# The feed-forward products of a hybrid block by Strassen's scheme: seven block products in place of eight

## The chip, the cores and the metric

The kernel runs on one core of a Trainium2 chip. The metric is the device time of one execution in microseconds, as the median of three runs. A core has a tensor engine (PE), a vector engine (DVE), a scalar engine (ACT) and a general engine (POOL), each with an instruction queue of its own that is worked off in order, and a queue for transfers (SP). All four engines work on the on-chip memory SBUF. PE writes its products to PSUM, from where DVE and ACT read them.

## The reference

A stack of two layers works on 512 tokens of 1024 features. Each layer has a feed-forward part (FFN), a mixer and a second FFN:

```python
def rms_norm(x, w):
    xf = x.astype(jnp.float32)
    y = xf * lax.rsqrt(jnp.mean(xf * xf, axis=-1, keepdims=True) + NORM_EPS)
    return (y * w.astype(jnp.float32)).astype(x.dtype)

def swiglu_ffn(x, w_gate, w_up, w_down):
    return (jax.nn.silu(x @ w_gate) * (x @ w_up)) @ w_down

for l in range(DEPTH):
    x = x + 0.5 * swiglu_ffn(rms_norm(x, ffn1_norm_w[l]), ffn1_w_gate[l], ffn1_w_up[l], ffn1_w_down[l])
    x = x + hybrid_mixer(rms_norm(x, mix_norm_w[l]), ...)
    x = x + 0.5 * swiglu_ffn(rms_norm(x, ffn2_norm_w[l]), ffn2_w_gate[l], ffn2_w_up[l], ffn2_w_down[l])
```

The hidden width of an FFN is 2816. The mixer joins an mLSTM, a state-space model and a differential attention. Everything is float32.

## The kernel before, in words

The residual stream x lies feature-major: eight tiles x[d] of 128 features by 512 tokens. A float32 product is made of three products of a faster kind (float32r). Each operand is split into a high part, which is its cast, and a low part, which is the rest; `mm3` (lines 125 to 128) adds high x high, high x low and low x high into one PSUM bank. `prep` splits x (lines 133 and 134: xh, xl) and multiplies the norm's gain in; the root mean square is divided out behind the product. Weights come by `load` (1 MiB each, two buffers `raw`) and are split by `split` in pieces of 1024 columns: ACT casts to `whi` (line 120), DVE subtracts to `wlo` (line 121).

`ffn` runs over 22 tiles f of the hidden width. For each it makes gate and up (8 steps of k each, so 24 products of 128x128 by 128x512 each), then DVE and ACT form silu(gate) * up and split it into gh and gl (lines 203 to 214). Then it runs over the eight output tiles d, with 22 steps of k each, and adds to x[d] (line 227). POOL has nothing to do in an FFN. In the first FFN `build_bias` makes a table for the attention, which one transfer from POOL's queue writes to the chip's main memory (line 252).

A scheduler sets the order in each queue when the program is built; blocks under `tc.high_priority()` (loads and splits) go ahead where they can. A tile waits for its slot, which the pool's number of buffers (`bufs`) and its `tag` decide.

## Time and profile before

| what | value |
|---|---|
| median of 3 runs | 2030.84 us (2029.91 to 2032.18) |
| span of the profiled execution | 2028.7 us |
| busy PE | 1990.6 us, 98% |
| busy DVE, ACT, POOL | 50%, 35%, 5% |
| mean granted clock of PE | 0.992 |

The span runs from the first to the last instruction of the profiled execution; its time in the runs is 2.1 us more in the median. Busy time of PE is the union of its products, which overlap: one lasts longer than the distance to the next start. The start-to-start distance tells what one costs in a row of them. In the rows below, "L121" is line 121 of the kernel, "wlo<-raw,whi" are output and inputs, and a bracket behind a row is the idle time of the engine ahead of it and what ended it. The duration of a DVE or POOL instruction is from its start to its end in the record, with any time that it stood inside.

### The profile page before, as it was taken

How to read it: one execution, taken by the hardware profiler on the slowest of the kernel's cores; microseconds unless marked ns; L12 is line 12 of the kernel's file. 1: busy time of each engine (PE TensorE's matmuls, PEld its weight loads, DVE VectorE, ACT ScalarE, POOL GpSimd, SP SyncE). 2: the span in 40 equal slices, each digit the busy share in tenths (PEclk: the TensorE clock that was granted, in tenths of full speed). 3: DMA queues.
4: the chain of work that ended last, by engine and by line, in shares of the span. 5: the costliest groups of instructions: out<-in, count | busy, mean ns of one | idle time of the engine just before them, and what ended most of it. 6: DMA issues, size and time to landing. Idle time of an engine off the chain costs nothing.

```text
span 2028.7 us, 23646 instructions
## 1 busy us (share of the span) xinstructions
PE 1990.6 (98%) x9654; PEld 1662.2 (82%) x9654; DVE 1014.5 (50%) x1659; ACT 700.9 (35%) x1144; POOL 110.1 (5%) x133
## 2 busy tenths in 40 slices
PE   8999999999899999999999999999998999999999
PEld 6878888978788888888888888889787888888887
DVE  6444433478766444443344444333876754444321
ACT  5223222345554333222232332223464533332211
POOL 0000000132210000000000000001222100000000
PEclk9999999999999999999999999999998999999999
DMA  5332222344212222222222222223532022222321
GB/s 177 95 118 83 104 103 85 118 144 127 83 52 81 86 104 85 103 104 83 104 84 103 104 84 104 103 75 122 159 110 88 32 99 89 104 85 103 109 99 62
DMA packets 35064, 200.73 MB, mean 99 GB/s; under 512 B 5179, under 2 KB 5467, under 8 KB 14092
## 3 DMA queue, kind: packets, MB, share of 16 engines
q1 hardware_dynamic: 29756, 185.28, 26.2%
q0 software_dynamic: 5200, 13.95, 2.8%
q8 instruction: 75, 1.23, 0.2%
q14 instruction: 33, 0.27, 0.0%
HBM read 191.56 MB, written 7.65 MB: 98 GB/s over the span
## 4 chain that ended last, share of the span: by engine, by line
PE 92%; DVE 4%; DMA 3%; ACT 1%; issue 1%; SPq 0%; POOL 0%; ACTq 0%; DVEq 0%; POOLq 0%
PE acc L126 16%; PE acc L128 16%; PE acc L127 16%; PE aux L126 12%; PE aux L128 12%; PE aux L127 12%; DMA raw<-wgu 3%; PE aux L764 1%; PE aux L643 1%; PE po L555 1%; PE po L755 0%; PE aux L544 0%; PE aux L523 0%; PE side L755 0%; ACT whi L120 0%
## 5 line engine op out<-in xcount | busy, mean ns | idle before, releaser
L120 ACT CAST whi<-raw 128x1024 fp32r<-128x1024 f32 (+2 forms) x344 | 350.8, 1022 | 994.2 <-PE acc L127 407.3
L121 DVE TENSOR_TENSOR wlo<-raw,whi 128x1024 fp32r<-128x1024 f32 (+1 forms) x326 | 386.2, 1187 | 346.1 <-ACT whi L120 345.6
L126 PE MATMUL acc<-xh,whi 128*128 128x512 f32 x896 | 353.1, 394 | 12.8 <-ACT xh L133 8.2
L127 PE MATMUL acc<-xl,whi 128*128 128x512 f32 x896 | 352.5, 393 | 0.0
L128 PE MATMUL acc<-xh,wlo 128*128 128x512 f32 x896 | 352.3, 393 | 0.1
L126 PE MATMUL aux<-xh,whi 128*128 128x512 f32 x704 | 274.2, 389 | 0.0
L128 PE MATMUL aux<-xh,wlo 128*128 128x512 f32 x704 | 274.1, 389 | 0.0
L127 PE MATMUL aux<-xl,whi 128*128 128x512 f32 x704 | 274.1, 389 | 0.0
L126 PEld LDWEIGHTS acc<-xh,whi 128*128 128x128 f32 x896 | 169.4, 189 | 47.3 <-ACT xh L133 8.2
L128 PEld LDWEIGHTS acc<-xh,wlo 128*128 128x128 f32 x896 | 169.1, 189 | 34.7 <-DVE wlo L121 1.1
L127 PEld LDWEIGHTS acc<-xl,whi 128*128 128x128 f32 x896 | 169.4, 189 | 34.0 <-DVE xl L134 0.4
L207 DVE TENSOR_TENSOR us<-aux,rsb 128x512 f32<-128x512 f32 x88 | 60.8, 691 | 265.7 <-PE aux L128 265.7
L127 PEld LDWEIGHTS aux<-xl,whi 128*128 128x128 f32 x704 | 132.3, 188 | 27.6
L128 PEld LDWEIGHTS aux<-xh,wlo 128*128 128x128 f32 x704 | 132.3, 188 | 27.5
L126 PEld LDWEIGHTS aux<-xh,whi 128*128 128x128 f32 x704 | 132.3, 188 | 27.4
L204 DVE TENSOR_TENSOR gs<-acc,rsb 128x512 f32<-128x512 f32 x88 | 60.8, 691 | 176.4 <-PE acc L128 172.5
L126 PE MATMUL acc<-gh,whi 128*128 128x512 f32 x352 | 138.7, 394 | 0.0
L126 PE MATMUL aux<-gh,whi 128*128 128x512 f32 x352 | 138.7, 394 | 0.0
L128 PE MATMUL acc<-gh,wlo 128*128 128x512 f32 x352 | 138.0, 392 | 0.0
L128 PE MATMUL aux<-gh,wlo 128*128 128x512 f32 x352 | 138.0, 392 | 0.0
L127 PE MATMUL acc<-gl,whi 128*128 128x512 f32 x352 | 136.6, 388 | 0.0
L127 PE MATMUL aux<-gl,whi 128*128 128x512 f32 x352 | 136.6, 388 | 0.0
(265 smaller groups left out, 2668.4 us busy)
## 6 DMA issues: line engine op xcount, KB each, us to landing
raw<-wgu SPq DMA_DIRECT2D x87, 1024.0 KB, 4.8
raw<-wdn SPq DMA_DIRECT2D x44, 1024.0 KB, 4.8
raw<-win SPq DMA_DIRECT2D x12, 1024.0 KB, 4.9
raw<-winf SPq DMA_DIRECT2D x12, 1024.0 KB, 4.9
raw<-wout SPq DMA_DIRECT2D x8, 1024.0 KB, 4.8
st<-qk_dram POOLq DMA_DIRECT2D x24, 256.0 KB, 5.4
qk_dram<-hl POOLq DMA_DIRECT2D x16, 256.0 KB, 3.3
sS<-row_dram SPq DMA_DIRECT2D x8, 512.0 KB, 4.4
```

What stands on the lines that cost most here:

```text
L120: act.copy(hi[:, t], raw[:, lo:lo + n])
L121: eng.tensor_tensor(lw[:, t], raw[:, lo:lo + n], hi[:, t].bitcast(F32), ALU.subtract)
L126: pe.matmul(out, lh, rh, start=first, stop=False)
L127: pe.matmul(out, lh, rl, start=False, stop=False)
L128: pe.matmul(out, ll, rh, start=False, stop=last)
L204: dve.tensor_tensor(gs, pp[0], rsb, ALU.mult)
L207: dve.tensor_tensor(us, pp[1], rsb, ALU.mult)
L555: pe.matmul(po[:, h * 64:(h + 1) * 64], at["a", n][:, j * P:(j + 1) * P], dv[j][:, (2 * p + h) * 64:(2 * p + h + 1) * 64], start=j == 0, s ...
L643: pe.matmul(py[:, j * P + hh * 64:j * P + hh * 64 + 64], sS[:, hh * S + j * P:hh * S + (j + 1) * P], XC[:, j, h * 64:(h + 1) * 64], start= ...
L764: pe.matmul(pnv[:, n, :], D[:, off[j] + (n - j) * P:off[j] + (n - j + 1) * P], V[:, j, h, :], start=j == 0, stop=j == n)
```

## The change

Gate, up and down products are made as products of 2x2 blocks. A block is 128 features by 128 hidden features (of a weight matrix) or 128 rows by 256 tokens (of x or of the hidden values h). A product of two such 2x2 arrays takes eight block products; the scheme takes seven, with sums of blocks as operands (the form with few sums by Winograd). The seven are named in STEPS: 11, s1, s2, s4, s3, 12, 22. The weights' operands are the loaded blocks 11, 12, 22 and the sums s1 = 21 + 22, s2 = s1 - 11, s3 = 11 - 21, s4 = 12 - s2, which POOL makes (`form`), 1024 columns each, in a pool of three buffers. Each of the seven is then split as before. The moving operands are three blocks of x and four sums of blocks (xR, xT, made by `prep7`), or of h (hR, hT, made behind each pair of hidden tiles, with POOL for the sums). Each product is 256 columns wide.

`gate_up(p)` makes the pair p of hidden tiles (11 pairs), gate and up in turn in each step. PSUM results are added on: ACT copies four of the seven running sums out (sn), and DVE and POOL add them to the outputs. `down(c, j)` makes half j of the output features from the chunk c of three pairs (two in the last), and adds to x with small instructions on DVE and POOL. Chunks run between the pairs: down(0, .) behind pair 3, down(1, .) behind pair 6, down(2, 0) behind pair 9, and the rest at the end.

`load` now brings 512 KiB in four buffers, one per block; whi and wlo have four buffers in place of three. In the mixer loads are cut the same way and some tiles move to other slots. `build_bias` takes its tiles from the slots "cg" and "cu" of the FFN, where "cu" has one buffer.

```diff
     def load(src, soon=True):
         n = src.shape[1]
         with tc.high_priority() if soon else nullcontext():
-            raw = wp.tile([P, 2 * WPC], F32, name="raw", tag="raw", bufs=2)
+            raw = wp.tile([P, WPC], F32, name="raw", tag="raw", bufs=4)
             nc.sync.dma_start(out=raw[:, :n], in_=src)
         return raw
 
...
     def split(raw, lo, n, eng=dve):
-            hi = wp.tile([P, WPC], F32R, name="whi", tag="whi", bufs=3)
-            lw = wp.tile([P, WPC], F32R, name="wlo", tag="wlo", bufs=3)
+            hi = wp.tile([P, WPC], F32R, name="whi", tag="whi", bufs=4)
+            lw = wp.tile([P, WPC], F32R, name="wlo", tag="wlo", bufs=4)
+            act.copy(hi[:, :n], raw[:, lo:lo + n])
+            eng.tensor_tensor(lw[:, :n], raw[:, lo:lo + n], hi[:, :n].bitcast(F32), ALU.subtract)
...
+    def prep7(i, wcol, tmp, four):
+        if i == 0:
+            parts["xR"] = [handed(4 + n, [P, 4, 2, 256], F32R, f"xR{n}") for n in range(3)]
+            parts["xT"] = []
+        xT = handed(i, [P, 4, 2, 256], F32R, "xT")
+        parts["xT"].append(xT)
+        xw = four("xw")
+        for n in range(2):
+            w = pv[:, wcol + 2 * i + n:wcol + 2 * i + n + 1]
+            act.activation(xw[:, 2 * n:2 * n + 2].rearrange("p a b -> p (a b)"), x[2 * i + n], AF.Copy, scale=w)
+        for n, b in enumerate((0, 2, 3)):
+            r = parts["xR"][n][:, i]
+            act.copy(r[:, 0], xw[:, b])
+            dve.tensor_tensor(r[:, 1], xw[:, b], r[:, 0].bitcast(F32), ALU.subtract)
+        sums(four("xt"), xw, xT, dve)
+        for n in range(2):
+            square(2 * i + n, tmp)
+    def sums(t, b, out, eng):
+        eng.tensor_tensor(t[:, 0], b[:, 1], b[:, 0], ALU.subtract)
+        eng.tensor_tensor(t[:, 1], b[:, 3], t[:, 0], ALU.subtract)
+        eng.tensor_tensor(t[:, 2], b[:, 3], b[:, 1], ALU.subtract)
+        eng.tensor_tensor(t[:, 3], b[:, 2], t[:, 1], ALU.subtract)
+        act.copy(out[:, :, 0], t)
+        dve.tensor_tensor(out[:, :, 1], t, out[:, :, 0].bitcast(F32), ALU.subtract)
...
-    def ffn(l, which, nxt, first):
...
+    STEPS = (("11", 0, "X"), ("s1", 3, "Y"), ("s2", 4, "X"), ("s4", 2, "Y"), ("s3", 5, "X"), ("12", 1, "Z"), ("22", 6, "X"))
+    def seven(raws, n, pair_w, np_, spool, fpool, rhs, done, after=None):
+        forms = {}
+        def form(name):
+            if name in raws:
+                src = raws[name]
+            else:
+                a, b, op, eng = {
+                    "s1": (raws["21"], raws["22"], ALU.add, pool),
+                    "s2": (forms.get("s1"), raws["11"], ALU.subtract, pool),
+                    "s4": (raws["12"], forms.get("s2"), ALU.subtract, pool),
+                    "s3": (raws["11"], raws["21"], ALU.subtract, pool),
+                }[name]
+                with tc.high_priority():
+                    src = spool.tile([P, WPC], F32, name=name, tag="S", bufs=3)
+                    eng.tensor_tensor(src[:, :n], a[:, :n], b[:, :n], op)
+                forms[name] = src
+            return split(src, 0, n)
+        ps, copies = {}, {}
+        nk = pair_w // P
+        for name, f, where in STEPS:
+            hi, lw = form(name)
+            for s in range(np_):
+                new = (s, where) not in ps
+                if new:
+                    ps[s, where] = acc() if where == "X" else aux()
+                out = ps[s, where][:, 0:256]
+                for k in range(nk):
+                    c = slice(s * pair_w + k * P, s * pair_w + (k + 1) * P)
+                    r = rhs(f, k)
+                    mm3(out, hi[:, c], lw[:, c], r[:, 0], r[:, 1], new and k == 0, k == nk - 1, True)
+                if name in ("11", "s1", "s2", "s3"):
+                    t = fpool.tile([P, 256], F32, name="sn", tag="sn", bufs=8)
+                    act.copy(t, out)
+                    copies[s, name] = t
+                done(s, name, out, copies)
+            if after:
+                after(name)
+    def ffn(l, which, nxt, first, ctx3):
+        wcol = l * PV_N + (PV_N2 if which else PV_N1)
+        fp = ctx3.enter_context(tc.tile_pool(name=f"f{l}{which}", bufs=1, reuse_waits="tile"))
...
+        def gate_up(p):
+            raws = raw11 if first and p == 0 else {b: load(aps["wgu"][l, which, p, n]) for n, b in ((0, "11"), (2, "21"), (3, "22"), (1, "12"))}
+            c = [four("cg"), fp.tile([P, 4, 256], F32, name="cu", tag="cu")]
+            def done(s, name, out, copies):
+                if name == "s4":
+                    dve.tensor_tensor(c[s][:, 1], out, copies[s, "s2"], ALU.add)
+                elif name == "s3":
+                    pool.tensor_tensor(c[s][:, 3], copies[s, "s3"], copies[s, "s1"], ALU.add)
+                elif name == "12":
+                    dve.tensor_tensor(c[s][:, 0], out, copies[s, "11"], ALU.add)
+                elif name == "22":
+                    act.copy(c[s][:, 2], out)
+            def after(name):
+                if p == 0 and name == "s1":
+                    spread(rms_of_x())
+            seven(raws, 1024, 512, 2, fp, fp, x_of, done, after)
+            cg, cu = c
+            flat = [t.rearrange("p (m n) t -> p m (n t)", m=2) for t in c]
+            rb = rsb[:, None, :].broadcast_to([P, 2, S])
+            dve.tensor_tensor(flat[0], flat[0], rb, ALU.mult)
+            pool.tensor_tensor(flat[1], flat[1], rb, ALU.mult)
+            act.activation(cg, cg, AF.Silu)
+            dve.scalar_tensor_tensor(cu, cg, 0.5, cu, ALU.mult, ALU.mult)
+            hR = fp.tile([P, 3, 2, 256], F32R, name="hR", tag="hR", bufs=4)
+            hT = fp.tile([P, 4, 2, 256], F32R, name="hT", tag="hT", bufs=4)
+            act.copy(hR[:, 0, 0], cu[:, 0])
+            act.copy(hR[:, 1:3, 0], cu[:, 2:4])
+            dve.tensor_tensor(hR[:, 0, 1], cu[:, 0], hR[:, 0, 0].bitcast(F32), ALU.subtract)
+            dve.tensor_tensor(hR[:, 1:3, 1], cu[:, 2:4], hR[:, 1:3, 0].bitcast(F32), ALU.subtract)
+            sums(four("ht"), cu, hT, pool)
+            hF[p] = hR, hT
+        def down(c, j):
+            ps = range(3 * c, min(3 * c + 3, 11))
+            n = len(ps) * P
+            src = aps["wd3"][l, which, c, j] if c < 3 else aps["wd2"][l, which, j]
+            raws = {b: load(src[m]) for m, b in ((0, "11"), (2, "21"), (3, "22"), (1, "12"))}
+            def h_of(f, k):
+                hR, hT = hF[ps[k]]
+                return hR[:, f] if f < 3 else hT[:, f - 3]
+            L, R = slice(0, 256), slice(256, 512)
+            def done(s, name, out, copies):
+                xa, xb = x[2 * (2 * j + s)], x[2 * (2 * j + s) + 1]
+                if name == "11":
+                    pool.tensor_tensor(xa[:, L], xa[:, L], copies[s, "11"], ALU.add)
+                elif name == "s1":
+                    pool.tensor_tensor(xb[:, R], xb[:, R], copies[s, "s1"], ALU.add)
+                elif name == "s2":
+                    pool.tensor_tensor(xa[:, R], xa[:, R], copies[s, "s2"], ALU.add)
+                elif name == "s4":
+                    dve.tensor_tensor(xa[:, R], xa[:, R], out, ALU.add)
+                elif name == "s3":
+                    dve.tensor_tensor(xb[:, R], xb[:, R], copies[s, "s3"], ALU.add)
+                elif name == "12":
+                    dve.tensor_tensor(xa[:, L], xa[:, L], out, ALU.add)
+                elif name == "22":
+                    dve.tensor_tensor(xb[:, L], xb[:, L], out, ALU.add)
+                    if c == 3:
+                        i = 2 * j + s
+                        if nxt is None:
+                            for d in (2 * i, 2 * i + 1):
                                 nc.sync.dma_start(out=aps["out"][:, d, :], in_=x[d])
+                        elif nxt[0] == "mx":
+                            for d in (2 * i, 2 * i + 1):
+                                prep(d, nxt[1], tmp)
+                        else:
+                            prep7(i, nxt[1], tmp, four)
+            seven(raws, 2 * n, n, 2, fp, fp, h_of, done)
+        for p in range(11):
+            gate_up(p)
+            if p == 2 and first:
+                build_bias(fp)
+            if p in (3, 6):
+                down(p // 3 - 1, 0)
+                down(p // 3 - 1, 1)
+            if p == 9:
+                down(2, 0)
+        down(2, 1)
+        down(3, 0)
+        down(3, 1)
...
+    def build_bias(bp):
+        oh = bp.tile([P, 1024], F32, name="oh", tag="cg", bufs=2)[0:33, 0:NREL]
+        nc.sync.dma_start(out=oh, in_=aps["oh"])
+        rb = tp.tile([33, 4], F32, name="rb")
+        dve.memset(rb, NEG)
+        nc.sync.dma_start(out=rb[0:32], in_=aps["rel_bias"])
+        dve.tensor_scalar(rb, rb, -1.0, None, ALU.mult)
+        row = bp.tile([P, 1024], F32, name="brow", tag="cu")[0:4, 0:NREL]
+        for a, b in ((0, 320), (320, 640)):
+            ps = aux()
+            pe.matmul(ps[0:4, :b - a], rb, oh[:, a:b], start=True, stop=True)
+            dve.tensor_copy(row[:, a:b], ps[0:4, :b - a])
+        pool.dma_start(out=bias_dram, in_=row[:, None, :].broadcast_to([4, P, NREL]))
```

The first place is POOL's queue in an FFN. In the kernel before, the rows around the FFNs are these (bias_dram is the table's transfer; Gm, Ps and T belong to the mixer):

```order
L252 DMA bias_dram_128<-row_549 512x1x640
L461 MEMSET Gm_2975 128x64
L468 MEMSET Ps_2981 128x4
L509 DMA T_3021<-bias_dram_128 128x512
L121 ISA
```

In the changed kernel the queue between pair 2's first sum and its end in the first FFN holds these rows (s1 to s4 the weight sums of pair 2; cg, cu the gate and up of pair 1; ht its sums of h):

```order
L221 TENSOR_TENSOR s1_801<-raw_759,raw_761 128x1024
L221 TENSOR_TENSOR s2_837<-s1_801,raw_757 128x1024
L284 TENSOR_TENSOR cg_504<-sn_660,sn_559 128x256
L221 TENSOR_TENSOR s4_871<-raw_763,s2_837 128x1024
L284 TENSOR_TENSOR cu_505<-sn_675,sn_574 128x256
L221 TENSOR_TENSOR s3_903<-raw_757,raw_759 128x1024
L299 TENSOR_TENSOR cu_505<-cu_505,rsb_93 128x1024
L162 TENSOR_TENSOR ht_750<-cu_505 128x256
L164 TENSOR_TENSOR ht_750<-cu_505 128x256
L163 TENSOR_TENSOR ht_750<-cu_505,ht_750 128x256
L165 TENSOR_TENSOR ht_750<-cu_505,ht_750 128x256
```

POOL had one instruction in an FFN and now has eleven for each pair.

The second place is DVE's queue in an FFN. Before, these rows stand around one hidden tile:

```order
L212 TENSOR_TENSOR gl4_565<-us_561,gh4_564 128x512
L204 TENSOR_TENSOR gs_628<-acc_574,rsb_106 128x512
L121 TENSOR_TENSOR wlo_670<-raw_638,whi_669 128x1024
L207 TENSOR_TENSOR us_631<-aux_603,rsb_106 128x512
L208 TENSOR_TENSOR us_631<-us_631,gs_628 128x512
L121 TENSOR_TENSOR wlo_711<-raw_708,whi_710 128x1024
L212 TENSOR_TENSOR gl5_635<-us_631,gh5_634 128x512
```

In the changed kernel these rows stand between the splits of pair 2 (wlo_840 of s2, wlo_874 of s4, wlo_906 of s3, wlo_940 of block 12, wlo_972 of block 22) and the end of pair 1 (cg_504, cu_505, hR_744, hT_745):

```order
L286 TENSOR_TENSOR cg_504<-aux_682,sn_523 128x256
L286 TENSOR_TENSOR cu_505<-aux_696,sn_538 128x256
L108 TENSOR_TENSOR wlo_840<-s2_837,whi_839 128x1024
L298 TENSOR_TENSOR cg_504<-cg_504,rsb_93 128x1024
L108 TENSOR_TENSOR wlo_874<-s4_871,whi_873 128x1024
L301 SCALAR_TENSOR_TENSOR cu_505<-cg_504,cu_505 128x1024
L108 TENSOR_TENSOR wlo_906<-s3_903,whi_905 128x1024
L306 TENSOR_TENSOR hR_744<-cu_505,hR_744 128x256
L307 TENSOR_TENSOR hR_744<-cu_505,hR_744 128x2x256
L167 TENSOR_TENSOR hT_745<-ht_750,hT_745 128x4x256
L108 TENSOR_TENSOR wlo_940<-raw_763,whi_939 128x1024
L108 TENSOR_TENSOR wlo_972<-raw_761,whi_971 128x1024
```

The split of blocks 12 and 22 stands behind the whole end of the pair ahead, and so do the loads that wait for the slots of blocks 12 and 22.

The third place is the transfer queue at the start of the program. Before:

```order
L83 DMA pv_107<-pv 128x148
L89 DMA raw_111<-wgu 128x512
L90 DMA x0_81<-xT 128x512
L89 DMA raw_111<-wgu 128x512
L90 DMA x1_82<-xT 128x512
L90 DMA x2_83<-xT 128x512
L89 DMA raw_111<-wgu 128x512
L90 DMA x3_84<-xT 128x512
L89 DMA raw_111<-wgu 128x512
L90 DMA x4_85<-xT 128x512
L90 DMA x5_86<-xT 128x512
```

In the changed kernel (raw_106, raw_116, raw_118, raw_120 are blocks 11, 21, 22, 12 of pair 0, raw_496 and raw_498 blocks 11 and 21 of pair 1):

```order
L260 DMA pv_94<-pv 128x148
L100 DMA raw_106<-wgu 128x1024
L100 DMA raw_116<-wgu 128x1024
L100 DMA raw_118<-wgu 128x1024
L100 DMA raw_120<-wgu 128x1024
L263 DMA x0_84<-xT 128x512
L263 DMA x1_85<-xT 128x512
L263 DMA x2_86<-xT 128x512
L263 DMA x3_87<-xT 128x512
L263 DMA x4_88<-xT 128x512
L263 DMA x5_89<-xT 128x512
L100 DMA raw_496<-wgu 128x1024
```

All weights of the first pair now stand ahead of x, and two loads of the second pair stand ahead of x6 and x7.

## Rows read from the trace of the kernel before

**Rows 1.** The page, part 1: busy time of each engine
```profile
PE 1990.6 (98%) x9654; PEld 1662.2 (82%) x9654; DVE 1014.5 (50%) x1659; ACT 700.9 (35%) x1144; POOL 110.1 (5%) x133
```

**Rows 2.** Windows by stage: busy us (instructions) of PE, PEld, DVE, ACT, POOL; clock; DMA
```profile
0.00:380.40 380.40, 367.36 (x1604) 300.89 (x1605) 164.52 (x210) 116.27 (x147) 1.48 (x5) 1.00 0.33 108
380.40:658.90 278.50, 267.83 (x1626) 232.07 (x1625) 197.85 (x447) 138.95 (x314) 54.32 (x64) 0.98 0.32 102
658.90:1021.40 362.50, 362.50 (x1602) 299.10 (x1602) 155.23 (x191) 106.57 (x131) 0.00 (x0) 1.00 0.28 96
...
1662.40:2028.70 366.30, 362.62 (x1601) 298.87 (x1599) 144.56 (x175) 95.86 (x112) 0.00 (x0) 1.00 0.26 93
```

**Rows 3.** Timeline of PE, 28 products of 512 columns: start, length
```profile
343.79 0.39 PE L128 MATMUL aux<-gh,wlo 128*128 128x512 f32 x1
...
349.97 0.39 PE L128 MATMUL aux<-gh,wlo 128*128 128x512 f32 x1
```

**Rows 4.** The same, 98 products of 256 columns in the mixer
```profile
394.75 0.28 PE L127 MATMUL acc<-wlo,xh 128*128 128x256 f32 x1
...
406.39 0.28 PE L128 MATMUL acc<-whi,xl 128*128 128x256 f32 x1
```

**Rows 5.** Groups of DVE by shape: count, busy us, mean ns
```profile
L121 DVE TENSOR_TENSOR wlo<-raw,whi 128x1024 fp32r<-128x1024 f32 x304 | 371.4, 1223 | 323.2 <-ACT whi L120 322.7
L121 DVE TENSOR_TENSOR wlo<-raw,whi 128x512 fp32r<-128x512 f32 x16 | 10.5, 686 | 11.1 <-ACT whi L120 11.1
L756 DVE TENSOR_TENSOR D<-po,D 128x256 f32<-128x256 f32 x8 | 3.3, 418 | 3.2 <-PE po L755 3.2
```

**Rows 6.** Groups of ACT by shape
```profile
L120 ACT CAST whi<-raw 128x1024 fp32r<-128x1024 f32 x320 | 336.3, 1052 | 948.9 <-PE acc L127 400.8 <-issue 311.6 <-PE aux L127 173.5
L657 ACT COPY bt<-aux 128x256 f32<-128x256 f32 x6 | 2.2, 365 | 5.9 <-PE aux L655 5.9
```

**Rows 7.** Two lines on POOL: ns min/median/max, shapes
```profile
L121 POOL TENSOR_TENSOR wlo<-raw,whi x18: 1373/2386/2644, 381.4 to 1548.5; 128x1024 fp32r<-128x1024 f32 x16, 128x544 fp32r<-128x544 f32 x2
L742 POOL TENSOR_TENSOR D<-row,cn x32: 452/456/902, 563.8 to 1603.7; 128x128 f32<-128x128 f32 x32
```

**Rows 8.** Timeline of DVE and POOL around three instructions of POOL
```profile
423.93 2.39 POOL L121 TENSOR_TENSOR wlo<-raw,whi 128x1024 fp32r<-128x1024 f32 x1 [14.37 <-ACT whi L120]
424.01 2.40 DVE L155 SCALAR_TENSOR_TENSOR ssq<-rs_q,ssq 128x64 f32<-128x64 f32 x1
426.44 0.22 DVE L153 TENSOR_TENSOR rs_q<-ssq 128x64 f32<-128x64 f32 x1
...
448.90 2.39 POOL L121 TENSOR_TENSOR wlo<-raw,whi 128x1024 fp32r<-128x1024 f32 x1 [2.89 <-ACT whi L120]
449.44 0.68 DVE L613 TENSOR_TENSOR YS<-side,bc 128x512 f32<-128x512 f32 x1
450.04 1.80 DVE L585 SCALAR_TENSOR_TENSOR xs<-rw,cwh,xs 128x512 f32<-128x512 f32 x1
...
535.07 1.22 DVE L121 TENSOR_TENSOR wlo<-raw,whi 128x1024 fp32r<-128x1024 f32 x1
535.63 2.89 POOL L631 TENSOR_TENSOR sS<-sS,cn 128x1024 f32<-128x1024 f32 x1 [19.84 <-DMA sS<-row_dram]
```

**Rows 9.** DMA issues: count, size, median us to landing
```profile
raw<-wgu SPq DMA_DIRECT2D x87, 1024.0 KB, 4.8
raw<-win SPq DMA_DIRECT2D x4, 544.0 KB, 3.6
bias_dram<-row POOLq DMA_DIRECT2D x1, 1280.0 KB, 56.5
```

**Rows 10.** Timeline: first product
```profile
8.20 0.79 PE L126 MATMUL acc<-xh,whi 128*128 128x512 f32 x1 [8.20 <-ACT xh L133]
```

**Rows 11.** Windows in the mixer, ten us each
```profile
550.00:560.00 10.00, 6.57 (x46) 6.32 (x46) 9.41 (x14) 5.73 (x17) 5.16 (x2) 0.86 0.15 55
560.00:570.00 10.00, 10.00 (x57) 9.95 (x57) 3.05 (x5) 3.12 (x10) 2.07 (x5) 0.63 0.32 105
```

More of the change, by code (lines that the diff above doesn't have):

```diff
@@ L71, in hybrid_kernel, with handed @@
     x = [res.tile([P, S], F32, name=f"x{d}") for d in range(KD)]
[L72 to L73 removed]
     sqacc = res.tile([P, S], F32, name="sqacc")
     rsb = res.tile([P, S], F32, name="rsb")
+    def handed(n, shape, dtype, name):
+        return hand.tile(shape, dtype, name=name, tag=f"a{n}")
+    parts = {}
     pv = const.tile([P, DEPTH * PV_N], F32, name="pv")
@@ new lines, in ffn, with four, tmp, x_of @@
+    def ffn(l, which, nxt, first, ctx3):
+        wcol = l * PV_N + (PV_N2 if which else PV_N1)
+        fp = ctx3.enter_context(tc.tile_pool(name=f"f{l}{which}", bufs=1, reuse_waits="tile"))
+        def four(name):
+            return fp.tile([P, 4, 256], F32, name=name, tag="cg", bufs=2)
+        def tmp():
+            return four("sq").rearrange("p a b -> p (a b)")[:, 0:S]
+        if first:
+            raw11 = {}
+            with tc.high_priority():
+                nc.sync.dma_start(out=pv, in_=aps["pv"])
+                raw11["11"] = load(aps["wgu"][l, which, 0, 0])
+                for d in range(KD):
+                    nc.sync.dma_start(out=x[d], in_=aps["xT"][:, d, :])
+                for n, b in ((2, "21"), (3, "22"), (1, "12")):
+                    raw11[b] = load(aps["wgu"][l, which, 0, n])
+                nc.sync.dma_start(out=cn, in_=aps["cn"])
+                nc.sync.dma_start(out=bc, in_=aps["bc"])
+            for i in range(4):
+                prep7(i, wcol, tmp, four)
+        xR, xT = parts["xR"], parts["xT"]
+        hF = {}
+        def x_of(f, k):
+            return xR[f][:, k] if f < 3 else xT[k][:, f - 3]
+        def gate_up(p):
[58 more added lines that the diff above has]
+                            for d in (2 * i, 2 * i + 1):
+                                nc.sync.dma_start(out=aps["out"][:, d, :], in_=x[d])
+                        elif nxt[0] == "mx":
[16 more added lines that the diff above has]
+        down(3, 1)
@@ L811, in w_out @@
             if d not in wo:
-                if d % 2 == 0:
-                    wcache["out"] = load(aps["wout"][l, d // 2])
-                wo[d] = split(wcache["out"], d % 2 * 1024, 1024) + (aux() if d % 2 else acc(),)
+                raw = load(aps["wout"][l, d // 2][:, d % 2 * 1024:(d % 2 + 1) * 1024])
+                wo[d] = split(raw, 0, 1024) + (aux() if d % 2 else acc(),)
             hi, lw, ps = wo[d]
@@ L823, in w_out @@
                     nc.sync.dma_start(out=aps["out"][:, d, :], in_=x[d])
-                else:
-                    prep(d, nxt)
+                elif nxt[0] == "mx":
+                    prep(d, nxt[1], tmp0)
+                elif d % 2:
+                    prep7(d // 2, nxt[1], tmp0, four)
         for d in range(2):
```

203 lines of the change are left out of this document (63 added, 140 removed).

## The prediction, made before the changed kernel ran

> **What bounds the kernel now.** I read the page's busy shares first: PE is busy 98% of the span, DVE half, ACT a third, POOL a twentieth [rows 1]. Then the windows by stage, to see where each engine works [rows 2]. An FFN takes 362.5 us and PE is busy in all of it; the first takes 380.4 (it begins with the loads), the last 366.3 (it ends with the output). POOL does nothing there. The two mixers take 278.5 each (the row left out, 1021.4 to 1662.4, is one FFN and one mixer more: 641.0). So an FFN is bound by PE alone, and there the timeline gives the price of a product: 28 starts of 512 columns from 343.79 to 349.97, 0.229 us apart [rows 3]. 1584 of them (22 tiles x 16 x 3 and 8 x 22 x 3) make 362.6: the whole stage.
>
> **PE's part.** The mixer shows the width that the change uses: 98 products of 256 columns start 0.120 us apart, each with its own weight load [rows 4]. After the change an FFN has 11 pairs x 168, six downs x 126 and two x 84, in all 2772 products, or 332.6 us: 30 us less per FFN, 120 for the four. Half the width costs 52%, so of the eighth that the scheme saves two thirds are left. [...]
>
> **Who shares what.** Next I looked for what the work moved to DVE and POOL meets. In the mixer both run at the same time, and the timeline shows it [rows 8]. At 424.01 a DVE instruction of 64 columns, whose like takes 0.22, starts while a POOL tensor_tensor runs (423.93 to 426.32), and takes 2.40: it ends 0.09 behind POOL. At 450.04 one of 512 columns takes 1.80 and ends 0.55 behind POOL. Both read two tensors from SBUF. The one at 449.44, with an input from PSUM, takes its 0.68 in the middle of the same POOL instruction. It works the other way too: at 535.63 POOL starts beside a split on DVE and takes 2.89 in place of 2.39. So POOL's tensor_tensor and a DVE instruction with two SBUF inputs run one after the other. [...]
>
> **One pair of hidden tiles.** POOL gets five instructions of 1024 columns (four weight sums, the norm's factor) at 2.39 and six of 256. For these I interpolate between 0.456 at 128 and 1.373 at 544 columns: 0.74 [rows 7]. Sum 5 x 2.39 + 6 x 0.74 = 16.4. DVE gets ten of 1024 with two SBUF inputs (seven splits, the norm's factor for gate, silu x up, the low part of hT) at 1.22, two for hR of 0.42 and 0.69, sum 13.3; and four of 256 from PSUM at 0.42, 1.7 [rows 5]. ACT gets nine of 1024 at 1.05, ten PSUM copies at 0.37 and two casts for hR, 14.1 [rows 6]. PE needs 168 x 0.120 = 20.2. Each engine alone would fit beside PE. But POOL and DVE exclude each other: 16.4 + 13.3 = 29.7. A change of hands hides about 0.15 of the next instruction (0.55 for 0.69, and 0.50 of wait where DVE had 0.66 left [rows 8]); some 16 changes give 2.4 back: 27.3.
>
> On top of that come gaps in which neither can run, read from the queues shown with the change. Count from the end of the split of block 22. Only then is its buffer free, and the next pair's block 22 is loaded: 512 KiB, which I put at 3.5 from 3.6 for 544 KiB (4.8 for 1 MiB) [rows 9]. POOL's first sum s1 needs it and heads POOL's queue; DVE has one split (1.22) beside it: gap 2.3. At the end of the pair the low part of hT stands on DVE ahead of the splits of blocks 12 and 22, and waits for four POOL sums and ACT's cast (1.1). Those splits then wait for ACT, which has its casts and three PSUM copies (1.2 together). Adding 1.1 for a dozen hand-overs between queues, gaps come to 5.7 and a pair to 33.0. PE waits 12.8 of it.
>
> **The other blocks.** Seven of the eleven pairs carry the end of the pair ahead (1, 2, 3, 5, 6, 8, 9): 231. The downs behind pairs 3, 6 and 9 carry one too: POOL 4 x 1.85 + 6 x 0.74 for the down (768 columns between 1.37 and 2.39) and 6.8 for the end, DVE 7 x 0.95 + 0.8 and 4.8, together 30.9, less 2.6 for changes, plus 1.7 of gap: 30.0 each, 90. The downs without (0,1) and (1,1) cost 19 each (11.8 + 7.5 - 1.5 + 1.2), 38. Pairs 4, 7 and 10 stand behind such a down or have their end in the next; their lock sum is 18 and PE sets 20.4: 61. Down (2,1) takes 24, and (3,0), (3,1) with 512 columns 17.5 and 19.5 (the last with the next stage's norm): 61. Pair 0 takes 20 plus 5, in which PE waits for the last quarter of prep7: 25. An FFN is 506, against 362.5.
>
> **Once in the program.** At the start PE begins at 8.20 now [rows 10]. After it, four weight blocks go ahead of x, ACT and DVE take the weight sums first, and then prep7 costs about 5 on either engine for each of four quarters; s1's operand of the last quarter comes at about 42, pair 0's last split at 49 instead of 25 behind a stage's begin: 24, say 25. The bias table's transfer takes 56.5 to land [rows 9]. It now reads from the slot "cu", which pair 3's up results need. It is issued some 6 before the end of pair 3, and they are wanted 12 behind it, so DVE, ACT and POOL stand at that place for about 37 (bounds: 0 if it lands as fast as a weight load, 45). The hand-overs into the mixers cost some 8 together, the last output 4.
>
> **Sum.** Mixers 557 (their instructions stay), FFNs 4 x 506 = 2024, 25 + 37 + 8 + 4 = 74: 2655. This is a span to set against 2028.7; the median of the runs stood 2.1 above that, which I leave out.
>
> **The bounds of the unknown.** The changed FFN has no like in the trace for the alternation of two full queues. Low: no gaps at all, pairs at 27.3, downs at 28.3 and 18, rest a little shorter: 450 per FFN, 2430. High: nothing hidden at the changes and twice the hand-overs, 36.5 per pair and 32 per down: 545 per FFN, 2810. I take the middle since the order in the queues forces the gaps, and the changes are measured.
>
> **Rivals.** *The engines run side by side, and PE sets the time*: 4 x 338 + 557 + 45, about 1950, faster. For it: every engine alone is under PE's 20.2 per pair, and loads are ahead. Against: three collisions in rows 8, in both directions. It decides if less than half of the 13.3 on DVE is excluded by POOL. 5%. *The lock alone*: queues always have something ready and gaps close, 2430. For it: there are three to four buffers at each step. Against: hT ahead of the split of block 22, and the load behind it. 15%. [...] 12%. *Something between the first two* (only part excluded), 1950 to 2430: 3%.
>
> **Numbers.** The forecast has 65%: 2655, by itself 2550 to 2780. With the rivals, 2430 to 2840 holds 8 in 10. Under 0.2% (4 us) cannot be told from no change here. Faster comes from the first rival alone: 5%; the same: 1%; slower: 94%.
>
> **What would show it.** Right: PE's share in the FFNs falls to some 65%; POOL's weight sums and DVE's splits are recorded at 3 us and more where each would take 2.4 and 1.2, with no two of them ending without one waiting; PE's waits end with DVE's wlo; pairs with an end ahead take 33, pairs 4 and 7 about 20; one stand of some 37 us at pair 3, with the table's transfer as releaser. Wrong: DVE's splits stay at 1.22 beside running POOL sums; or PE stands less than 8 us per pair; or PE's clock in FFNs is under 0.7.

## The result and the profile after

The changed kernel takes 2662.64 us (median of 4 runs, 2658.79 to 2663.68), the kernel before 2030.38 beside it: 1.311 times as long, interval 1.309 to 1.313. Forecast were 2655, between 2430 and 2840. The first part of the page of the changed kernel, busy time of each engine [rows 1]:

```profile
PE 2075.1 (78%) x14406; PEld 1969.3 (74%) x14406; DVE 1883.0 (71%) x2283; ACT 1182.1 (44%) x2164; POOL 1518.2 (57%) x937
```

The windows by stage, columns as in [rows 2]: first FFN, mixer, two FFNs, mixer, last FFN.

```profile
0.00:577.00 577.00, 395.65 (x2786) 382.80 (x2787) 376.60 (x356) 234.93 (x397) 349.47 (x206) 0.84 0.23 70
577.00:857.00 280.00, 267.05 (x1634) 230.26 (x1633) 204.69 (x474) 145.99 (x330) 54.04 (x64) 0.99 0.34 102
857.00:1877.00 1020.00, 764.26 (x5571) 750.31 (x5570) 739.31 (x666) 443.32 (x752) 706.05 (x402) 0.85 0.21 68
1877.00:2157.50 280.50, 266.79 (x1633) 230.37 (x1632) 204.57 (x474) 146.37 (x330) 54.12 (x64) 0.99 0.34 102
2157.50:2661.90 504.40, 381.36 (x2790) 375.62 (x2788) 357.82 (x315) 211.48 (x357) 354.54 (x201) 0.85 0.21 70
```

The mixers are as before (280 for 278.5). An FFN takes 504 to 510 where it took 362.5, the first one 577. PE, which was busy all the time, now stands a quarter of it.

Lines in the rows are those of the changed kernel: L107 is a split's cast and L108 its low part, L112 to L114 are the three products of `mm3`, L162 to L167 the sums of h and their split, L221 the weight sums, L240 a copy out of PSUM, L282 to L299 the additions and the norm's factor, L301 silu x up.

Here is one pair in the second FFN, from silu x up of pair 4 to that of pair 5: the end of pair 4, blocks 12 and 22 of pair 5, and the first weight sums of pair 6. POOL, then DVE from the timeline (start, length; most rows are left out):

```profile
1068.77 0.72 POOL L165 TENSOR_TENSOR ht<-cu,ht 128x256 f32<-128x256 f32 x1
1076.67 2.40 POOL L221 TENSOR_TENSOR s<-raw 128x1024 f32<-128x1024 f32 x1 [7.18 <-DMA raw<-wgu]
1079.15 3.28 POOL L221 TENSOR_TENSOR s<-s,raw 128x1024 f32<-128x1024 f32 x1
...
1084.07 2.41 POOL L221 TENSOR_TENSOR s<-raw,s 128x1024 f32<-128x1024 f32 x1
1086.44 1.73 POOL L284 TENSOR_TENSOR cu<-sn 128x256 f32<-128x256 f32 x1
1088.12 3.38 POOL L221 TENSOR_TENSOR s<-raw 128x1024 f32<-128x1024 f32 x1
1091.47 3.33 POOL L299 TENSOR_TENSOR cu<-cu,rsb 128x1024 f32<-128x1024 f32 x1
...
1063.75 1.23 DVE L301 SCALAR_TENSOR_TENSOR cu<-cg,cu 128x1024 f32<-128x1024 f32 x1 [2.23 <-POOL cu L299]
...
1084.10 3.46 DVE L108 TENSOR_TENSOR wlo<-s,whi 128x1024 fp32r<-128x1024 f32 x1
1087.49 1.76 DVE L298 TENSOR_TENSOR cg<-cg,rsb 128x1024 f32<-128x1024 f32 x1
1089.17 3.42 DVE L108 TENSOR_TENSOR wlo<-s,whi 128x1024 fp32r<-128x1024 f32 x1
...
1094.83 1.23 DVE L301 SCALAR_TENSOR_TENSOR cu<-cg,cu 128x1024 f32<-128x1024 f32 x1 [2.24 <-POOL cu L299]
```

Two splits here take 3.4 where one alone takes 1.22 [rows 5], and two of POOL's sums 3.3 for 2.39. The ends show that each stands inside its record while the other works: the split from 1084.10 ends at 1087.56, 1.08 behind the sum that ran beside it, and the sum from 1088.12 ends at 1091.50, 2.25 behind DVE's instruction of 1087.49. Between silu x up of pair 4 (1063.75) and of pair 5 (1094.83) lie 31.1 us. Adding up the intervals of the timeline, POOL's records cover 22.4 of them, those of DVE with two SBUF inputs 21.0, both at once 15.9, at least one 27.5, and in 3.6 there is none. The forecast was 27.3 of work one after the other and 5.7 of gaps. The groups by shape (count, then busy us and mean ns) show it over the whole program, with instructions that met nothing in the same mean:

```profile
L108 DVE TENSOR_TENSOR wlo<-s,whi 128x1024 fp32r<-128x1024 f32 x176 | 406.1, 2310 | 68.6 <-ACT whi L107 68.0
L221 POOL TENSOR_TENSOR s<-raw 128x1024 f32<-128x1024 f32 x88 | 251.0, 2852 | 406.8 <-DMA raw<-wgu 251.2 <-PE aux L114 112.1 <-DVE wlo L108 35.0
```

Where PE stands in the second FFN is in the view of waits (us in total, times, longest), and the timeline of ACT and PE tells why:

```profile
PE acc L112 <- ACT sn L240: 55.6, 9, 9.6
PE acc L112 <- DVE x L338: 26.5, 7, 5.6
```

```profile
1069.52 1.04 ACT L166 CAST hT<-ht 128x1024 fp32r<-128x1024 f32 x1 [3.58 <-POOL ht L165]
1070.47 0.37 ACT L240 COPY sn<-acc 128x256 f32<-128x256 f32 x1
...
1070.89 0.58 PE L112 MATMUL acc<-xT,whi 128*128 128x256 f32 x1 [9.61 <-ACT sn L240]
...
1073.64 1.04 ACT L107 CAST whi<-raw 128x1024 fp32r<-128x1024 f32 x1 [1.04 <-PE acc L113]
```

In a pair with an end PE has one long stop, 7 to 10 us, mostly between the gate half and the up half of the products of s2. It waits for copies of finished sums out of PSUM, and these stand behind the cast of hT on ACT, which waits for POOL's last sum of h.

### The profile page after: what moved, and what is told of

Its sections match the earlier page's. It is cut to its first block, busy times and chain, and to the rows that moved or that the text cites. A ratio compares the mean times of both kernels' runs of the same rounds, so it can differ in the third digit from the quotient of the medians.

```text
span 2661.9 us, 36922 instructions
## 1 busy us (share of the span) xinstructions
PE 2075.1 (78%) x14406; PEld 1969.3 (74%) x14406; DVE 1883.0 (71%) x2283; ACT 1182.1 (44%) x2164; POOL 1518.2 (57%) x937
## 4 chain that ended last, share of the span: by engine, by line
PE 38%; POOL 27%; DVE 18%; issue 7%; DMA 5%; ACT 5%; another core or an unknown queue 1%; POOLq 0%; SPq 0%; ACTq 0%; DVEq 0%
POOL s L221 10%; PE acc L112 8%; DVE wlo L108 7%; PE acc L113 7%; PE acc L114 7%; POOL cu L299 5%; PE aux L112 4%; PE aux L113 4%; PE aux L114 4%; DMA raw<-wgu 4%; ACT whi L107 3%; POOL ht L162 3%; DVE x L334 2%; DVE cu L301 2%; POOL ht L163 2%
## 5 line engine op out<-in xcount | busy, mean ns | idle before, releaser
L221 POOL TENSOR_TENSOR s<-raw 128x1024 f32<-128x1024 f32 (+2 forms) x152 | 378.1, 2488 | 578.0 <-DMA raw<-wgu 251.2
L108 DVE TENSOR_TENSOR wlo<-s,whi 128x1024 fp32r<-128x1024 f32 (+2 forms) x304 | 585.1, 1927 | 131.9 <-ACT whi L107 131.0
L108 DVE TENSOR_TENSOR wlo<-raw,whi 128x1024 fp32r<-128x1024 f32 (+3 forms) x282 | 384.3, 1365 | 205.2 <-ACT whi L107 204.1
L107 ACT CAST whi<-s 128x1024 fp32r<-128x1024 f32 (+2 forms) x304 | 283.9, 936 | 495.7 <-POOL s L221 265.9
L112 PE MATMUL acc<-xT,whi 128*128 128x256 f32 x1056 | 318.9, 302 | 232.5 <-ACT sn L240 232.5
L107 ACT CAST whi<-raw 128x1024 fp32r<-128x1024 f32 (+3 forms) x300 | 284.9, 951 | 245.9 <-PE aux L113 147.0
L112 PEld LDWEIGHTS acc<-xT,whi 128*128 128x128 f32 x1056 | 216.5, 205 | 239.0 <-ACT sn L240 238.7
L113 PE MATMUL acc<-xT,whi 128*128 128x256 f32 x1056 | 313.0, 296 | 0.0
L114 PE MATMUL acc<-xT,wlo 128*128 128x256 f32 x1056 | 312.8, 296 | 0.0
L112 PE MATMUL aux<-xR,whi 128*128 128x256 f32 x704 | 211.5, 300 | 13.7 <-ACT sn L240 13.7
L113 PEld LDWEIGHTS acc<-xT,whi 128*128 128x128 f32 x1056 | 217.4, 206 | 0.0
L114 PEld LDWEIGHTS acc<-xT,wlo 128*128 128x128 f32 x1056 | 217.2, 206 | 0.0
L113 PE MATMUL aux<-xR,whi 128*128 128x256 f32 x704 | 209.5, 298 | 0.0
L114 PE MATMUL aux<-xR,wlo 128*128 128x256 f32 x704 | 208.5, 296 | 0.0
L221 POOL TENSOR_TENSOR s<-s,raw 128x1024 f32<-128x1024 f32 (+2 forms) x76 | 201.1, 2646 | 5.9
L240 ACT COPY sn<-acc 128x256 f32<-128x256 f32 x456 | 167.3, 370 | 66.9 <-PE acc L114 64.0
L112 PE MATMUL acc<-xR,whi 128*128 128x256 f32 x352 | 109.9, 315 | 101.8 <-DVE x L338 76.7
L221 POOL TENSOR_TENSOR s<-raw,s 128x1024 f32<-128x1024 f32 (+2 forms) x76 | 180.5, 2375 | 4.3 <-DMA raw<-wd 1.6
L112 PE MATMUL aux<-hR,whi 128*128 128x256 f32 x352 | 112.1, 318 | 85.1 <-ACT sn L240 66.9
L112 PE MATMUL acc<-hT,whi 128*128 128x256 f32 x528 | 164.7, 312 | 12.8 <-ACT sn L240 11.0
L113 PE MATMUL acc<-hT,whi 128*128 128x256 f32 x528 | 162.2, 307 | 0.0
L114 PE MATMUL acc<-hT,wlo 128*128 128x256 f32 x528 | 161.6, 306 | 0.0
```

What stands on the lines that cost most here:

```text
L107: act.copy(hi[:, :n], raw[:, lo:lo + n])
L108: eng.tensor_tensor(lw[:, :n], raw[:, lo:lo + n], hi[:, :n].bitcast(F32), ALU.subtract)
L112: pe.matmul(out, lh, rh, start=first, stop=False, skip_group_check=skip)
L113: pe.matmul(out, lh, rl, start=False, stop=False, skip_group_check=skip)
L114: pe.matmul(out, ll, rh, start=False, stop=last, skip_group_check=skip)
L221: eng.tensor_tensor(src[:, :n], a[:, :n], b[:, :n], op)
```

## Experiments

Theory: POOL's tensor_tensor and DVE's instructions with two SBUF inputs run one after the other; their sum and the gaps that the order of the queues forces make a pair. Rivals: both run side by side and something else is slow (1); the order of the queues and the loads set the pair (2); PE's lower clock (0.85 granted in the second FFN) does (3).

**The weight sums on DVE**: `"s1": (raws["21"], raws["22"], ALU.add, dve)`, the same for s2, s3, s4.

> The four weight sums s1 to s4 of a block run on DVE; nothing else is changed. Theory (POOL's tensor_tensor and DVE's instructions with two SBUF inputs run one after the other, so a pair takes the sum of both plus gaps): a sum of 1024 columns costs the sum 1.22 in place of 2.39, a pair falls by 4 x 1.17 = 4.7 us, from 31.1 to some 26.5, a down by 4 x 0.9 = 3.6; with the pairs that PE sets anyway left out, 60 us per FFN: about 2420 us. DVE's splits, 2.31 in the mean for the operands that are sums, come back to 1.3. Rival 1 (the two run side by side, and POOL's own chain of sums is just too long): DVE has 19.9 per pair, PE 20.2 sets the time, about 2250. Rival 2 (the order of the queues and the loads set the pair, not the work): under 2% change.

Measured: 2399.41 us, ratio 1.182 (1.180 to 1.184). Some 2420 were expected. A pair (4 to 5, second FFN) takes 27.1, and 22.9 of it have a record of POOL or of DVE with two inputs. The sums moved from the idler engine to the busier one, and the pair lost 4.0 us of the 4.7 that the theory gives. The splits of sums took 1.57 in the mean: less than 2.31, though not the 1.3 expected. Rival 1 (2250) is missed by 150 us. The next version stands at the same pair time with less work, so here the order may have held the pair too, and the time alone is no proof against rival 1; the records above are.

**No weight sums**: in `form`, `name = {"s1": "21", "s2": "22", "s4": "12", "s3": "11"}.get(name, name)`.

> The four weight sums are left out: their products take the loaded blocks 21, 22, 12 and 11 as operands, so the products are as many as before but their values are not those of the reference. Theory (exclusion): 9.6 us of a pair's 27.4 go, POOL keeps 6.8 and DVE 13.3; with 20.2 of PE per pair PE sets the time again, FFNs of 370 to 400 us, 2130 to 2230 in all. Rival 2 (order of the queues: hT's sums, its cast and the splits behind them, and the loads behind these, 7.2 us of wait on POOL per pair): the ring stays, pairs take 26 and more, over 2450. Rival 3 (PE at its lower clock sets the pair): PE has the same products, no change by more than 5%.

Measured: 2307.8 us, ratio 1.137 (1.135 to 1.139). The theory's 2130 to 2230 fell, and so did rival 2's 2450 and more; rival 3, which allowed 5% of change, is out as the main cause, with 13% less than the changed kernel. Work covers only 18.9 of a pair now, but the pair takes 27.2: PE still stops 4.5 us in each, and rival 2 holds for this remainder. The timeline of PE at that stop:

```profile
928.58 0.28 PE L114 MATMUL acc<-xT,wlo 128*128 128x256 f32 x1
933.33 0.58 PE L112 MATMUL acc<-xT,whi 128*128 128x256 f32 x1 [4.47 <-ACT sn L241]
933.71 0.42 PE L113 MATMUL acc<-xT,whi 128*128 128x256 f32 x1
933.92 0.42 PE L114 MATMUL acc<-xT,wlo 128*128 128x256 f32 x1
```

After the stop 25 products, up to 938.6, start 0.21 apart, not 0.12. In the changed kernel products start 0.21 apart behind a stop too, and there the granted clock is 0.50: 12 products from 1070.90 to 1073.60, behind the stop of 9.61. So PE runs slower for these 25 products: 20.2 of products, 4.5 of stop and some 2.5 of slower products (an estimate from the distances) are the pair. So two limits lay close together: 27.5 by the work, and some 26 to 27 by the order (27.2 here, 25.9 with the copies below). Had the engines run side by side, the 1950 of the first rival of the prediction would hardly have come either; that is argued and not shown, since the exclusion is still at work in this version (for 5.1 us of the pair both engines have a record).

**Five load buffers**: `tag="raw", bufs=5`, and `tag="sn", bufs=6` for the room.

> Five load buffers in place of four (sn has six in place of eight, for the room). The next block 22 can then be loaded ahead of the splits of blocks 12 and 22, and s1 and s2 move ahead of the sums for hT in POOL's queue. Theory (lock sum plus gaps that the order forces): of a pair's 31.1 us neither engine works in 3.6; these go at most, 20 to 35 us per FFN, and the 27.5 that are the sum of both engines' work stay: 2520 to 2590. Rival 2 (the loads and the order set the pair): POOL's 7.2 us of wait go whole, the pair falls to 24 and the time to some 2400. Rival 4 (PE's stop of 9 us per pair behind ACT's copies sets the pair, and loads don't matter): no change.

Measured: 2644.50 us, ratio 1.303 (1.301 to 1.305): 18 us less, where 70 to 140 were expected. By the time alone this is nearest to the fourth rival (no change). The rows tell more: the gap moved. The sums s1 and s2 now stand ahead of h's sums on POOL, and ACT's cast of hT waits for these (longest 7.5 us, before 3.6), and PE's copies behind it:

```profile
ACT hT L166 <- POOL ht L165: 60.2, 10, 7.5
PE aux L112 <- ACT sn L240: 53.3, 8, 10.3
```

Of the pair 4 to 5 (30.4) work covers 27.7: what both engines do is unchanged, and it still fills nine tenths of the pair when the loads come earlier.

**Copies in place of sums on POOL**: `eng.tensor_copy(src[:, :n], a[:, :n])`.

> POOL's weight sums become copies of their first operand (one input in place of two), so the values are not those of the reference; order, sizes and waits stay. Theory in its narrow form (what excludes is a POOL instruction with two SBUF inputs against a DVE instruction with two): splits beside a copy take 1.22 again, the lock sum falls by 9.6 per pair and the time to 2130 to 2300, if a copy takes 2.4 or less. Theory in its wide form (any POOL instruction of this kind excludes): the splits stay at 2.3 in the mean beside the copies, and the time stays within 5% of 2660, or follows the length of the copies. Rival 1 (no exclusion): no change unless copies are shorter.

Measured: 2370.37 us, ratio 1.168 (1.165 to 1.170), 70 us above the range of the narrow form, but the splits are back near 1.22:

```profile
L108 DVE TENSOR_TENSOR wlo<-s,whi 128x1024 fp32r<-128x1024 f32 x176 | 226.5, 1290 | 114.2 <-ACT whi L107 114.0
L221 POOL COPY s<-raw 128x1024 f32<-128x1024 f32 x132 | 155.5, 1178 | 492.6 <-DMA raw<-wgu 290.8 <-PE aux L114 112.1 <-issue 51.4
```

Yet single rows speak for the wide form. Here a copy starts first, and DVE, whose instruction takes 1.22 alone, ends 1.07 behind it:

```profile
814.10 1.06 POOL L221 COPY s<-s 128x1024 f32<-128x1024 f32 x1
...
814.20 2.03 DVE L301 SCALAR_TENSOR_TENSOR cu<-cg,cu 128x1024 f32<-128x1024 f32 x1 [3.33 <-POOL cu L299]
```

A copy excludes too; it only takes 1.06 here where a sum takes 2.39. Four times the difference is 5.3, and from 27.5 that leaves 22.2 of work per pair; 22.4 are measured, in a pair of 25.9. My narrow form has 1.22 beside a copy, and the 2.03 does not agree with it.

**The bias row in a tile of its own**: `row = tp.tile([4, NREL], F32, name="brow")`.

> The row of the bias table gets a tile of its own in place of the slot cu; the transfer itself stays. As the prediction had it (the slot is held until the transfer has landed, and that is the whole stand): the 37 us go, measured 47 between the marks of pairs 2 and 3 beyond the usual 28, so 2615 to 2626. Rival (read from the changed trace: POOL stands 27.9 us for a weight load that lands late beside the transfer, and only then 16.4 for the slot): some 16 to 20 us go, 2643 to 2647, and the late load stays. Rival 2 (the load alone decides): no change.

Measured: 2648.71 us, ratio 1.303 (1.300 to 1.306): 14 us less, near the rival read from the trace, not the prediction's 37. POOL in the changed kernel, and its wait in this one:

```profile
146.08 1.28 POOL L383 DMA_DIRECT2D bias_dram<-brow  x1 [5.46 <-DVE brow L382]
175.22 1.79 POOL L221 TENSOR_TENSOR s<-raw 128x768 f32<-128x768 f32 x1 [27.86 <-DMA raw<-wd]
...
200.92 0.73 POOL L284 TENSOR_TENSOR cu<-sn 128x256 f32<-128x256 f32 x1 [16.41 <-DMA bias_dram<-brow]
```

```profile
POOL s L221 <- DMA raw<-wd: 29.6, 3, 27.5
```

The stand has two parts: weight loads that land late beside the transfer, and then the slot. Only the second went: 14 of the 47 us that the place takes beyond a usual pair.

**Eight products**, the scheme undone and the rest kept: `for i in range(2): for j in range(2): hi, lw = split(raws["12"[i] + "12"[j]], 0, n)`, each block times both halves of the tokens, and no sums.

> The scheme alone is undone: the same blocks, loads, chunks and 256-column products, but eight products of four blocks, no sums of weights, of x or of h, nothing on POOL. Theory (the sums on POOL and DVE are what costs): PE sets the time with 3168 products x 0.120 = 380 per FFN, a few us of hand-overs: 385 to 400, in all 2130 to 2200. Rival 2 (the order of queues, the small loads and the chunks between the pairs cost by themselves): over 2350.

Measured: 2166.47 us, ratio 1.067 (1.065 to 1.069). Three pairs and two downs take 103.7, which is 864 products x 0.120, without a stop:

```profile
754.00:1030.00 276.00, 276.00 (x2302) 276.00 (x2302) 121.34 (x192) 70.59 (x89) 0.00 (x0) 1.00 0.28 91
```

So 496 of the 632 us are the scheme's (2662.6 less 2166.5), although it has fewer products, and the rest of the rewrite costs 136. Of these the half width alone makes some 70 (380.2 less 362.6 per FFN, four times). Blocks, loads and chunks are not what is slow, and PE's granted clock is 1.00 in this stretch, where it isn't stopped.

**All tensor_tensor work on DVE**, POOL only casts hT: `dve` for `pool` in the sums, `flat[1]`, `c[s][:, 3]` and x; `cast=pool.tensor_copy` for hT.

> All tensor_tensor work of POOL in the FFNs goes to DVE (weight sums, sums of h, the norm's factor for up, additions to cg, cu and x); POOL does the cast of hT, with one input, in place of ACT. Theory (exclusion, so that POOL is worth nothing here and costs twice): DVE has some 21.4 per pair, a little over PE's 20.2; pairs of 23 to 24, downs of 16 to 17, FFNs of 385 to 405: 2160 to 2240. Rival 2 (order of queues): pairs of 26 as without the sums, 2300 and more. Rival 1 (side by side, POOL relieves DVE): slower than with the weight sums alone on DVE, over 2400.

Measured: 2223.88 us, ratio 1.095 (1.093 to 1.097). A pair takes 23.8, of which DVE's work with two inputs is 22.2 and neither engine works in 1.6. Taking POOL's sums and additions away is 439 us faster than using it for them, where rival 1 had over 2400: it is out. Of the 7.3 us that the pair lost, 5.3 are work and 2.0 gaps; the cast of hT left ACT's queue in the same edit, and no run takes it off ACT alone, so its own share isn't shown. DVE alone is still above PE's 20.2.

**Gate and up alone by the scheme**, sums on DVE; h is split as a whole and down made of plain products 512 wide, `mm3(ps_, w[m][0][:, cc], w[m][1][:, cc], gh[:, m], gl[:, m], ...)`; gh is cast on POOL, cu has two buffers, raw five, S four.

> One part alone: gate and up by the scheme with all sums on DVE, up's factor too; h is split as a whole (cast on POOL), and down is made of plain products of 512 columns from the same blocks and chunks; cu has two buffers, raw five, S four. Theory: PE 11 x 20.2 + 121 = 343 per FFN against 362.5; DVE 19.1 per pair, under PE; so the sums would be hidden, and FFNs take 350 to 375: 2010 to 2110. Rival 2 (the order of the queues stops PE once per pair, as where the sums were left out): pairs of 25 to 26, 2250 to 2300.

Measured: 2059.89 us, ratio 1.015 (1.013 to 1.016), inside the theory's 2010 to 2110. Three pairs take 60.5 us and the two downs of a chunk 33.6, PE without a stop, DVE busy for less:

```profile
817.60:878.10 60.50, 60.50 (x505) 60.47 (x504) 49.33 (x57) 32.46 (x52) 3.88 (x2) 1.00 0.28 90
878.10:911.70 33.60, 33.60 (x147) 27.04 (x146) 22.48 (x24) 8.56 (x10) 1.04 (x1) 1.00 0.36 122
```

Inside the pairs the seven products pay (20.2 for 23.0 of eight); what was left was at the starts and at the bias table.

**That version mended**: the table in eight transfers, `put_bias(brow, p - 2)` behind pairs 2 to 9; x loaded between the first blocks; the downs of the last chunks behind the last pair. And a second one with `pool.tensor_copy` for the casts of x.

> The version with gate and up alone by the scheme (2060), mended where its trace shows PE waiting: the bias table goes in eight transfers, one behind each of the pairs 2 to 9, from a tile of its own (PE lost some 29 us there); x is loaded between the first blocks (PE lost 35 of the first 60 us, 18 in the kernel before); the last two chunks of down stand behind the last pair, those of x0 to x3 first, so that the next norm begins 27 us ahead of the end (16 us lost between the FFNs). h has five buffers, S three. Theory (nothing else binds PE in these places): 25 + 8 + 8 us come back, some 2015 to 2025, a little under the kernel before. Rival (the pieces of the table slow the loads in eight places, or the h buffers hold up the last pairs): 2045 to 2070.

> As the mended version, with the casts of the norm's blocks of x (three of 256 columns, one of 1024 per quarter) on POOL in place of ACT. Theory (a POOL instruction with one input doesn't hold up DVE): ACT's part of a quarter falls from 4.6 to 2.5 us, DVE's 5.1 stays and sets it; 0 to 4 us less at each of the four places where x is prepared: 2005 to 2025. Rival (the casts hold up DVE's instructions as POOL's sums do): 5 to 15 us more than the mended version.

Measured: 2037.25 us, ratio 1.0028 (1.0018 to 1.0039), and 2042.66, ratio 1.0055 (1.0043 to 1.0068). The first is between theory and rival; the table's pieces did not spread, three of them went out together (the row at 128.35), and PE had 35.3 us of products in the first 60, where it had 34.7 in the version mended. The second is slower by 5, the low end of its rival (5 to 15); the first one's runs alone spread over 9 us, so the rows say more. POOL's casts of 256 columns took 618 ns in the mean where ACT took 397, and DVE's low parts behind them 476 where they took 418.

```profile
102.22 0.81 POOL L373 DMA_DIRECT2D bias_dram<-brow  x1 [14.57 <-DVE brow L369]
...
128.35 1.85 POOL L373 DMA_DIRECT2D bias_dram<-brow  x3
```

**The table from 128 partitions** (`pe.matmul(ps[:, :b - a], rb[:, h:h + 1].broadcast_to([33, P]), oh[:, a:b], ...)`, four transfers), slots of their own for xw and xt, and the sums of squares later.

> As the mended version (casts of x on ACT again), with two more places mended. The bias table: PE makes its row for 128 partitions (eight small products), ACT copies it, and four transfers read from 128 partitions in place of 4; PE lost some 12 us there to late weight loads. The norm: xw, xt and sq have slots of their own (h's, free at that time) in place of two shared ones, and the sums of squares go behind the preparation of x, up to the first pair's end. Theory (at the start ACT and DVE waited for these slots; the transfer is slow because it reads from 4 partitions): 5 to 8 us at the start, 6 to 10 at the table, 1 to 4 at each of the other three starts: 2012 to 2027, faster than the kernel before. Rival (DVE's work, 35 us for x and the first pair's sums, sets the start, whatever the slots): no more than 10 us in all, 2027 to 2034.

Measured: 2043.54 us, ratio 1.0066 (1.0053 to 1.0079), outside both ranges. The table held: each quarter landed in 2.5 us, and the first FFN ended at 385 and not 396. The later sums of squares lost more, at all four starts:

```profile
bias_dram<-brow POOLq DMA_DIRECT2D x4, 320.0 KB, 2.5
```

```profile
PE aux L194 <- DVE rst L180: 13.3, 4, 4.3
```

**The same with the sums of squares back in their place**, and the slots at the first start alone.

> The mended version (2037) with the bias table from 128 partitions (four transfers that landed in 2.5 us each, and no PE wait at that place: the first FFN ended at 385 in place of 396), with the sums of squares back inside the preparation of x, and the slots of their own for xw and xt at the first start alone. Theory (the later sums of squares made the other three starts longer, by 13.3 us of wait for rst): the 11 us of the first FFN stay and the other starts are those of the mended version: 2022 to 2029, just under the kernel before. Rival (the slots made them longer, or the starts differ by chance as the mended version's runs did, 2033 to 2042): 2030 to 2040.

Measured: 2021.18 us (2019.87 to 2023.87), ratio 0.9949 (0.9936 to 0.9963): faster than the kernel before by half a per cent, the only one of these that is. It is a us under the theory's range (2022 to 2029). All its runs lie below all those of the kernel before beside it (2029.37 to 2033.65). Its page, its first FFN and its second:

```profile
PE 1950.5 (96%) x12834; PEld 1773.0 (88%) x12834; DVE 1530.3 (76%) x2277; ACT 956.7 (47%) x1688; POOL 181.5 (9%) x180
```

```profile
0.00:385.00 385.00, 361.18 (x2411) 331.74 (x2412) 292.95 (x362) 183.25 (x290) 21.22 (x20) 1.00 0.32 107
...
664.00:1022.00 358.00, 351.90 (x2395) 326.92 (x2395) 283.55 (x342) 168.14 (x261) 17.81 (x11) 0.99 0.29 98
```

The gain lies in the two FFNs in the middle (358 for 362.5 here); the first is still longer than before (385 for 380.4).

Whether the slots or the squares cost the 22 us between the last two versions was not told apart; the 13.3 us of waits name the squares for part of it.

## Why the prediction was right, step by step

- *Who shares what* was right, and is the main reason of the result: 27.5 us per pair in which one or the other works, against 27.3. Work and gaps of the pair 4 to 5 were 27.5 + 3.6 in the changed kernel, 27.7 + 2.7 with five load buffers, 22.9 + 4.2 with the sums on DVE, 22.4 + 3.5 with the copies and 22.2 + 1.6 with all on DVE: the pair follows the work. Without the sums it does not (18.9 + 8.4); there the order sets it. The statement was too narrow in one point: a POOL copy excludes too (a DVE instruction of 1.22 took 2.03 beside one of 1.06).
- *The gaps* were 3.6 and not 5.7: 1.1 ahead of the low part of hT, 1.7 between the splits of blocks 12 and 22, 0.7 ahead of s1. The load for s1 was released at 1073.07, right behind the first of the two last splits, one split earlier than I had counted, so POOL's 7.18 of wait lay mostly beside DVE's work. Pairs 1, 2, 5 and 8 took 28.9 to 31.4 from silu x up to silu x up in the first two FFNs, and those just ahead of a down (3, 6 and 9, without the place of the table) 27.4 to 28.3, for the 33.0 of either.
- *The other blocks*: from silu x up of pair 4 to that of pair 7 I had 135.4 (two pairs, two downs, a pair behind them) and 135.6 are measured, but by errors that cancel: 58.5 for the first two pairs in place of 66, and 77.1 for the rest in place of 69.4. Pair 7 takes 28.3 from its first product (1161.25) to the next pair's, not 20.4: PE waits for its PSUM bank until the last add to x on DVE (5.6), and behind that stop its granted clock is 0.50 (1168.4 to 1172.6). An FFN came out at 504 to 510, forecast 506; that it is so near is luck in part.
- *Once in the program*: the first silu x up is at 72.4, in the second FFN 42.3 behind the stage's begin: 30 for the 25 of the start. The table's stand is 74.8 between the marks of pairs 2 and 3, where the second FFN has 27.8: 47 for 37, above the upper bound of 45. The step named the slot alone; three fifths of POOL's two long waits there were for late loads (27.9 and 16.4). Mixers had 560.5 for 557.
- *Sum*: FFNs 577 + 1020 + 504.4 = 2101.4 against 2024 + 74 = 2098; the span is 2661.9 against 2655.
- *What would show it*: the stand was there, ten us longer than said. Splits and sums at 3 us and more were only some: two of the seven splits between 1063.75 and 1094.83 and two of the four sums, and the splits of sums have 2.31 in the mean. Pair 7 was 28.3 and not about 20. PE's waits do not end with wlo but with ACT's copies behind the cast of hT, and PE's share in the FFNs is 75% (69% in the first) and not 65: its products would fill 65% at full speed (332.6 of 510), and the lower clock (0.85 granted) stretches them by some 50 us per FFN. So the clock fell, from the 1.00 of [rows 2], and it was not free. In a pair that PE sets, such as pair 7, it comes on top, some 2.5 us (28.3 less 20.2 and a wait of 5.6). In the pairs with an end most of it lies beside the work of POOL and DVE, but the gap of 1.7 ends when PE has passed the 12 products behind its stop (ACT's cast at 1073.64 waits for them), and these took 2.7 (1070.89 to 1073.62) at a granted clock of 0.50, where 1.4 is their time at 0.120. What it costs in all was not measured by itself; with no sums and no stops (eight products) the clock was 1.00.
- *The rivals*: side by side (1950) is out by the rows, where each record ends behind the other's, and by the version with all sums on DVE. The lock alone (2430) was not reached: five load buffers, which open the first of the gaps, gave 18 us. The 12% were for a fall of PE's clock that lengthens the FFNs by a tenth, to 2860: no run shows this tenth; the clock was 0.84 to 0.85 in the FFNs, and these took 2101.4 in all where the forecast has 2098.
